# The last layer norm of a transformer block: the final 512 columns in two parts, and one of four column blocks normalised by TensorE and ScalarE

## The chip, the cores and the metric

The kernel runs on one core of a Trainium2 chip. The metric is device time in microseconds of one execution. Three runs of the kernel before took 1463.31, 1463.54 and 1463.85 us; the median is 1463.54. The core has these engines, each with a queue of its own: TensorE (PE; its weight loads are shown as PEld), VectorE (DVE), ScalarE (ACT), GpSimd (POOL) and SyncE (SP), which here only issues transfers. They meet through semaphores.

## The reference

One block of a model of width 2048 on 256 tokens, in fp32: an input projection, two attention branches, an output projection, a layer norm, a gated feed-forward network of inner width 5632, and the last layer norm. The change touches only the last line and what delivers to it:

```python
def layer_norm(x, g, b):
    xf = x.astype(jnp.float32)
    mu = jnp.mean(xf, axis=-1, keepdims=True)
    var = jnp.mean(jnp.square(xf - mu), axis=-1, keepdims=True)
    return ((xf - mu) * lax.rsqrt(var + LN_EPS) * g.astype(jnp.float32) + b.astype(jnp.float32)).astype(x.dtype)
...
        h_gate, h_up = jnp.split(x @ w_ffn_in[l], 2, axis=-1)
        x = layer_norm(DEEPNORM_ALPHA * x + (jax.nn.silu(h_gate) * h_up) @ w_ffn_out[l], ln2_g[l], ln2_b[l])
```

## The kernel before

The 256 tokens are two blocks of 128 (`tb` 0 and 1), one token per partition. The 2048 output columns of the second feed-forward product are two groups `g` of 1024, each of two halves `n` of 512; column block j = 2g + n. Each product of fp32 values is made as three matmuls on rounded parts (`mm3`, lines 207 to 209: weights' high part, weights' low part, activations' low part), and the weights are streamed and split by ScalarE (line 83, `hi`) and VectorE (line 85, `lo`).

Group 1 is the last one. Its sums grow in four PSUM banks, `bank[2 * tb + n]`. Up to the last four pairs of weight chunks, each pair is used for both token blocks (`plain_pair`, or `seven_pair` for pairs done with seven products in place of eight). The last four pairs (`HELD = 4`) are used for block 0 as they arrive and kept in SBUF. So block 0 is ready first: its two banks are added to the residual `x1[0]` and its norm `ln2(0)` runs on VectorE, while TensorE goes through the kept chunks for block 1: 24 matmuls of 512 columns into `bank[2]`, then 24 into `bank[3]`. Each bank is added to `x1[1]` by `add_out` (line 1025), which also takes the statistics of the 512 columns (`bn_stats`, line 1028, one of four sets of six numbers).

The norm itself (`ln`): VectorE aggregates the four sets to mean and variance `mv` (line 1099), makes `first(0)`, (x - mean) * gamma (line 1089), adds epsilon (`ve`, line 1101), and GpSimd raises the sum to the power -0.5 (`rs`, line 412). Then come `second(0)`, x * rs + beta (line 1094), and the same two passes for column blocks 1, 2 and 3. Each finished column block is stored, alternately by ScalarE's and SyncE's queue (line 1335). Gamma and beta come broadcast to all 128 partitions in four tiles of 1024 columns (`ln2_t`, loaded by GpSimd, line 1306, in the middle of group 1).

TensorE and SyncE run in the order in which the code is written. For VectorE, ScalarE and GpSimd a scheduler sets the order, by the code's order, priorities (`tc.high_priority`) and dependencies; within an engine nothing overtakes at run time. Dependencies on a PSUM tile are kept for the whole bank.

## Time and profile before

| what | us |
|---|---|
| runs (three) | 1463.31, 1463.54, 1463.85 |
| profiled execution, first to last instruction (its own time is not shown beside it) | 1462.0 |
| TensorE busy, share of the span | 1447.7, 99% |
| VectorE busy | 1219.6, 83% |
| ScalarE busy | 797.0, 55% |
| GpSimd busy | 45.8, 3% |
| mean granted TensorE clock | 0.998 of full speed |

Times in the profile are microseconds from the span's start. A row of the timeline gives start, duration, engine, line of the kernel, operation, output <- inputs, shape, and in brackets the idle time of the engine before it with what ended it. Records of matmuls overlap: what one costs in a stream is the distance of the starts, not the duration. A row of a group gives, behind the count, busy time in us and the mean of one in ns.

### The profile page before, as it was taken

What the parts mean: (1) busy time and instruction counts of PE and PEld (TensorE: products, weight loads), DVE (VectorE), ACT (ScalarE), POOL (GpSimd) and SP (SyncE); (2) the same over time, 40 slices, a digit from 0 to 9 for tenths busy, and PEclk for the clock granted to TensorE, in tenths of its full rate; (3) what the DMA queues carried; (4) which work ended last, traced back from release to release, by engine and by line L of the source; (5) the groups of instructions that cost most, each with busy time, mean ns of one, the idle gap of its engine ahead of it and who ended that gap; (6) DMA issues with size and microseconds to landing.
All of it is one profiled execution on the core that took longest, in us unless ns stands there. A gap on an engine that the chain in (4) does not pass through costs nothing.

```text
span 1462.0 us, 19399 instructions
## 1 busy us (share of the span) xinstructions
PE 1447.7 (99%) x7146; PEld 1217.9 (83%) x7146; DVE 1219.6 (83%) x1654; ACT 797.0 (55%) x982; POOL 45.8 (3%) x58
## 2 busy tenths in 40 slices
PE   9999999999999999999999999999999999999996
PEld 9888888888888888888888888888888888888885
DVE  6798985468489678879886799989999998989887
ACT  6765443346466445545534565656566565554551
POOL 0002010030000000000000000000000000000000
PEclk9999999999999999999999999999999999999999
DMA  8646675444556565567856767666666667888853
GB/s 295 195 155 194 185 180 169 152 135 147 186 184 217 182 208 193 185 185 245 292 182 207 239 232 245 206 211 204 228 203 211 218 215 248 311 335 267 325 199 115
DMA packets 93407, 310.16 MB, mean 212 GB/s; under 512 B 16688, under 2 KB 17624, under 8 KB 92544
## 3 DMA queue, kind: packets, MB, share of 16 engines
q1 hardware_dynamic: 82176, 290.11, 59.5%
q0 software_dynamic: 4096, 16.45, 3.5%
q10 hardware_dynamic: 7040, 2.36, 0.7%
q8 instruction: 56, 0.92, 0.3%
q14 instruction: 39, 0.32, 0.1%
HBM read 295.05 MB, written 13.83 MB: 211 GB/s over the span
## 4 chain that ended last, share of the span: by engine, by line
PE 95%; DVE 2%; DMA 1%; issue 1%; ACT 1%; SPq 0%; POOLq 0%; DVEq 0%; ACTq 0%
PE acc L145 10%; PE acc L208 10%; PE acc L209 10%; PE acc L207 10%; PE aux L207 9%; PE aux L209 9%; PE aux L208 9%; PE acc L148 5%; PE acc L167 5%; PE acc L166 5%; PE acc L165 5%; PE aux L672 1%; PE aux L165 1%; PE aux L167 1%; PE aux L166 1%
## 5 line engine op out<-in xcount | busy, mean ns | idle before, releaser
L83 ACT CAST hi<-raw 128x1024 fp32r<-128x1024 f32 (+1 forms) x391 | 405.8, 1045 | 392.1 <-PE acc L167 88.2
L85 DVE TENSOR_TENSOR lo<-raw,hi 128x1024 fp32r<-128x1024 f32 (+1 forms) x391 | 473.8, 1220 | 148.0 <-ACT hi L83 145.1
L145 PE MATMUL acc<-X,hi 128*128 128x512 f32 x640 | 203.7, 399 | 0.0
L148 PEld LDWEIGHTS acc<-X,lo 128*128 128x128 f32 x640 | 120.2, 188 | 28.3
L207 PE MATMUL acc<-hi,X 128*128 128x512 f32 x364 | 142.2, 391 | 0.0
L209 PE MATMUL acc<-hi,X 128*128 128x512 f32 x364 | 141.7, 389 | 0.0
L208 PE MATMUL acc<-lo,X 128*128 128x512 f32 x364 | 141.7, 389 | 0.0
L207 PE MATMUL aux<-hi,X 128*128 128x512 f32 x332 | 129.9, 391 | 0.6 <-DVE ol__108 L852 0.6
L209 PE MATMUL aux<-hi,X 128*128 128x512 f32 x332 | 129.3, 389 | 0.0
L208 PE MATMUL aux<-lo,X 128*128 128x512 f32 x332 | 129.2, 389 | 0.0
L148 PE MATMUL acc<-X,lo 128*128 128x256 f32 x640 | 126.0, 278 | 0.0
L145 PEld LDWEIGHTS acc<-X,hi 128*128 128x128 f32 x640 | 97.5, 189 | 2.0 <-ACT hi L83 0.7
L240 ACT CAST f_thi<-f_wt 128x1024 fp32r<-128x1024 f32 x58 | 61.1, 1054 | 52.3 <-DVE f_wt L255 30.8
L165 PE MATMUL acc<-hi,X 128*128 128x512 f32 x224 | 89.6, 400 | 0.0
L167 PE MATMUL acc<-hi,X 128*128 128x512 f32 x224 | 87.4, 390 | 0.0
L166 PE MATMUL acc<-lo,X 128*128 128x512 f32 x224 | 87.3, 390 | 0.0
L209 PEld LDWEIGHTS acc<-hi,X 128*128 128x128 f32 x364 | 68.4, 188 | 14.3
L207 PEld LDWEIGHTS acc<-hi,X 128*128 128x128 f32 x364 | 68.4, 188 | 14.0
L208 PEld LDWEIGHTS acc<-lo,X 128*128 128x128 f32 x364 | 68.3, 188 | 13.9
L241 DVE TENSOR_TENSOR f_tlo<-f_wt,f_thi 128x1024 fp32r<-128x1024 f32 x58 | 70.2, 1220 | 6.3 <-ACT f_thi L240 6.0
L207 PEld LDWEIGHTS aux<-hi,X 128*128 128x128 f32 x332 | 62.3, 188 | 13.5 <-DVE ol__108 L852 0.8
L209 PEld LDWEIGHTS aux<-hi,X 128*128 128x128 f32 x332 | 62.3, 188 | 13.0
(545 smaller groups left out, 2883.2 us busy)
## 6 DMA issues: line engine op xcount, KB each, us to landing
raw<-in_wfg_dram SPq DMA_DIRECT2D x131, 512.0 KB, 4.1
raw<-in_wws_dram SPq DMA_DIRECT2D x80, 512.0 KB, 4.1
raw<-in_wfo_dram SPq DMA_DIRECT2D x70, 512.0 KB, 5.0
raw<-in_wgt_dram SPq DMA_DIRECT2D x52, 512.0 KB, 3.6
raw<-in_win_dram SPq DMA_DIRECT2D x37, 512.0 KB, 3.7
f_wraw<-in_wfg_dram SPq DMA_DIRECT2D x29, 512.0 KB, 5.9
wraw<-in_wfo_dram SPq DMA_DIRECT2D x18, 512.0 KB, 5.1
gt<-d_g SPq DMA_DIRECT2D x18, 512.0 KB, 6.3
```

Source lines behind the costliest of these rows:

```text
L83: nc.scalar.copy(hi, raw)
L85: nc.vector.tensor_sub(lo, raw, hi.bitcast(F32))
L145: nc.tensor.matmul(pss[c], hv[:, kk, cs[c]], X2[k // 4][:, k % 4], start=(k == 0), stop=False, skip_group_check=True)
L148: nc.tensor.matmul(pss[c][:, :S], lv[:, kk, cs[c]], xh[:, k, :], start=False, stop=(k == KT - 1), skip_group_check=True)
L165: nc.tensor.matmul(ps, xh, hv[:, kk], start=(k == 0), stop=False)
L166: nc.tensor.matmul(ps, xh, lv[:, kk], start=False, stop=False)
L167: nc.tensor.matmul(ps, xl, hv[:, kk], start=False, stop=(k == 2 * n - 1))
L207: nc.tensor.matmul(o, sh, hi, start=first, stop=False)
L208: nc.tensor.matmul(o, sh, lo, start=False, stop=False)
L209: nc.tensor.matmul(o, sl, hi, start=False, stop=last)
L240: nc.scalar.copy(hi, v)
L241: nc.vector.tensor_sub(lo, v, hi.bitcast(F32))
```

## The change

For block 1 the last bank is made in two parts of 256 columns: 24 matmuls for columns 0 to 255 of the bank, addition and statistics of these, then 24 for columns 256 to 511, addition and statistics. The statistics become five sets. Epsilon is added right behind the aggregate. Column block 0 of block 1 is final since group 0; it is multiplied by gamma ahead of time. Its rest, rs * (x gamma) - mean rs gamma + beta, is made by TensorE in one PSUM bank: a product with the diagonal matrix of rs, and a product of two rows per token (-mean * rs, and 1) with the two rows gamma and beta. ScalarE makes the column mean * rs and the diagonal, copies the transposed rows out of PSUM, copies the result out of PSUM and stores it. VectorE makes the two passes for column blocks 1, 2, 3 only, all three first passes ahead of the second passes; SyncE stores these. The argument `shut` only sets the flag that closes a bank's accumulation. Block 0 is normalised as before.

```diff
@@ -219,12 +219,12 @@
         cs = slice(n * 512, (n + 1) * 512)
         mm3(bank[2 * tb + n], sh[:, k, ts], sl[:, k, ts], hi[:, cs], lo[:, cs], q == 0 and j == 0, last and j == 1)
 
-    def plain_pair(bank, src, sh, sl, q, last):
+    def plain_pair(bank, src, sh, sl, q, last, shut=None):
         cks = pair_chunks(src, q)
         for j in range(2):
             for n in range(2):
                 for tb in range(NTB):
-                    plain(bank, cks, sh, sl, q, j, n, tb, last)
+                    plain(bank, cks, sh, sl, q, j, n, tb, last or 2 * tb + n == shut)
             tick()
 
     def seven_pair(bank, wbank, src, sh, sl, q, form, home, first, last):
@@ -1020,12 +1020,13 @@
         scaled(v21, m, OP.subtract)
         nc.vector.tensor_add(v22, v22, m)
 
-    def add_out(tb, g, n, ps):
-        v = out_block(tb, g, n)
-        nc.vector.tensor_add(v, v, ps)
-        if 2 * g + n == 0:
-            stats[tb] = sm.tile([P, 4, 6], F32, name="stats", tag="stats", bufs=2)
-        nc.vector.bn_stats(stats[tb][:, 2 * g + n, :], v)
+    def add_out(tb, g, n, ps, part=slice(0, 512)):
+        v = out_block(tb, g, n)[:, part]
+        nc.vector.tensor_add(v, v, ps[:, part])
+        j = 2 * g + n
+        if j == 0:
+            stats[tb] = sm.tile([P, 5, 6], F32, name="stats", tag="stats", bufs=2)
+        nc.vector.bn_stats(stats[tb][:, j + (part.start > 0), :], v)
 
     def load_x():
         for tb in range(NTB):
@@ -1096,7 +1097,7 @@
 
         with tc.high_priority(offset=ahead[0]):
             mv = sm.tile([P, 2], F32, name="mv", tag="mv", bufs=2)
-            nc.vector.bn_aggr(mv, stats[tb].rearrange("p a b -> p (a b)"))
+            nc.vector.bn_aggr(mv, stats[tb][:, :4].rearrange("p a b -> p (a b)"))
             ve = sm.tile([P, 1], F32, name="ve", tag="ve", bufs=2)
             nc.vector.tensor_scalar(ve, mv[:, 1:2], LN_EPS, None, op0=OP.add)
             rs = sm.tile([P, 1], F32, name="rs", tag="rs", bufs=2)
@@ -1294,7 +1295,7 @@
                 if q == WQ[g][-1]:
                     start(seven_chain(g, wbank, mp_.tile([P, 512], F32, name="wm", tag="wm")))
             else:
-                plain_pair(bank, wfo[g], hh_, hl_, q, q == FT // 2 - 1)
+                plain_pair(bank, wfo[g], hh_, hl_, q, q == FT // 2 - 1, 3 if g and q == n - 1 else None)
         return bank
 
 
@@ -1335,15 +1336,59 @@
         ln(tb, Halves(*ln2_t[:2]), Halves(*ln2_t[2:]), lambda j, v: (nc.sync if j % 2 else nc.scalar).dma_start(
             out[tb * P:(tb + 1) * P, j * 512:(j + 1) * 512], v))
 
+    ts1 = slice(P, S)
+
+    def held_part(n, part):
+        for q, cks in held:
+            for j in range(2):
+                k = 2 * q + (j + n) % 2
+                cs = slice(n * 512 + part.start, n * 512 + part.stop)
+                hi, lo = cks[j]
+                last = j == 1 and q == FT // 2 - 1
+                for a, b, end in ((hh_, hi, False), (hh_, lo, False), (hl_, hi, last)):
+                    nc.tensor.matmul(bank[2 + n][:, part], a[:, k, ts1], b[:, cs], start=False, stop=end,
+                                     skip_group_check=n == 1)
+        add_out(1, 1, n, bank[2 + n], part)
+
+    gt2, bt2 = (Halves(*ln2_t[i:i + 2]) for i in (0, 2))
+    v1 = [x1[1][:, j * 512:(j + 1) * 512] for j in range(4)]
+    rows2, turn = (hp_.tile([P, 1024], F32, name=n, tag=t) for n, t in (("rows2", "hH2"), ("turn", "hL2")))
+    for i, src in enumerate((ln2g, ln2b)):
+        nc.gpsimd.dma_start(rows2[i:i + 1, :512], bass.AP(tensor=src.tensor, offset=src.offset, ap=[[0, 1], [1, 512]]))
+    ct = sm.tile([P, 2], F32, name="ct")
+    nc.gpsimd.memset(ct, -1.0)
     for n in range(2):
         add_out(0, 1, n, bank[n])
     ln2(0)
-    for n in range(2):
-        for q, cks in held:
-            for j in range(2):
-                plain(bank, cks, hh_, hl_, q, j, n, 1, q == FT // 2 - 1)
-        add_out(1, 1, n, bank[2 + n])
-    ln2(1)
+    held_part(0, slice(0, 512))
+    nc.vector.tensor_mul(v1[0], v1[0], gt2[:, slice(0, 512)])
+    held_part(1, slice(0, 256))
+    held_part(1, slice(256, 512))
+
+    mv = sm.tile([P, 2], F32, name="mv", tag="mv", bufs=2)
+    ve = sm.tile([P, 1], F32, name="ve", tag="ve", bufs=2)
+    rs = sm.tile([P, 1], F32, name="rs", tag="rs", bufs=2)
+    diag, ctT = turn[:, :P], turn[0:2, 512:512 + P]
+    with tc.high_priority(offset=LEAD):
+        nc.vector.bn_aggr(mv, stats[1].rearrange("p a b -> p (a b)"))
+        nc.vector.tensor_scalar(ve, mv[:, 1:2], LN_EPS, None, op0=OP.add)
+        rsqrt(rs, ve, hv)
+        nc.scalar.activation(ct[:, 0:1], mv[:, 0:1], AF.Copy, scale=rs)
+        nc.scalar.activation(diag, ident, AF.Copy, scale=rs)
+    y, a = ps_aux(), ps_aux()
+    nc.tensor.transpose(a[0:2, :P], ct, ident)
+    nc.scalar.activation(ctT, a[0:2, :P], AF.Copy, scale=-1.0)
+    nc.tensor.matmul(y, diag, v1[0], start=True, stop=False)
+    nc.tensor.matmul(y, ctT, rows2[0:2, :512], start=False, stop=True)
+    for j in (1, 2, 3):
+        nc.vector.scalar_tensor_tensor(v1[j], v1[j], mv[:, 0:1], gt2[:, slice(j * 512, j * 512 + 512)],
+                                       op0=OP.subtract, op1=OP.mult)
+    for j in (1, 2, 3):
+        nc.vector.scalar_tensor_tensor(v1[j], v1[j], rs, bt2[:, slice(j * 512, j * 512 + 512)],
+                                       op0=OP.mult, op1=OP.add)
+        nc.sync.dma_start(out[P:, j * 512:(j + 1) * 512], v1[j])
+    nc.scalar.copy(v1[0], y)
+    nc.scalar.dma_start(out[P:, :512], v1[0])
     assert not chains
     fh.close()
```

The order changes at three places. First, VectorE at the end of the program, from the bank ahead of the last one on (`x_1` is block 1's residual, `acc` a PSUM bank, `ln_0`, `ln_1` gamma, `ln_2`, `ln_3` beta). Before:

```order
L1025 TENSOR_TENSOR x_1_10660<-x_1_10660,acc 128x512 [waits PE_49]
L1028 BN_STATS stats<-x_1_10660 128x6 [waits DVE_49]
L1025 TENSOR_TENSOR x_1_10660<-x_1_10660,acc 128x512 [waits PE_49]
L1028 BN_STATS stats<-x_1_10660 128x6 [waits DVE_49]
L1099 BN_AGGR mv<-stats 128x2 [waits DVE_49]
L1089 SCALAR_TENSOR_TENSOR x_1_10660<-x_1_10660,mv,ln_0_11748 128x512 [waits DVE_49]
L1101 TENSOR_SCALAR ve<-mv 128x1
L1089 SCALAR_TENSOR_TENSOR x_1_10660<-x_1_10660,mv,ln_0_11748 128x512
L1094 SCALAR_TENSOR_TENSOR x_1_10660<-x_1_10660,rs,ln_2_11932 128x512 [waits Pool_49]
L1094 SCALAR_TENSOR_TENSOR x_1_10660<-x_1_10660,rs,ln_2_11932 128x512 [waits DVE_49]
L1089 SCALAR_TENSOR_TENSOR x_1_10660<-x_1_10660,mv,ln_1_11834 128x512 x2
L1094 SCALAR_TENSOR_TENSOR x_1_10660<-x_1_10660,rs,ln_3_12018 128x512 [waits DVE_49] x2
```

Now:

```order
L1025 TENSOR_TENSOR x_1_10660<-x_1_10660,acc 128x512 [waits PE_49]
L1029 BN_STATS stats<-x_1_10660 128x6 [waits DVE_49]
L1025 TENSOR_TENSOR x_1_10660<-x_1_10660,acc 128x256 [waits PE_49]
L1029 BN_STATS stats<-x_1_10660 128x6 [waits DVE_49]
L1025 TENSOR_TENSOR x_1_10660<-x_1_10660,acc 128x256 [waits PE_49]
L1029 BN_STATS stats<-x_1_10660 128x6 [waits DVE_49]
L1373 BN_AGGR mv<-stats 128x2 [waits DVE_49]
L1374 TENSOR_SCALAR ve<-mv 128x1 [waits DVE_49]
L1384 SCALAR_TENSOR_TENSOR x_1_10660<-x_1_10660,mv,ln_0_11748 128x512
L1384 SCALAR_TENSOR_TENSOR x_1_10660<-x_1_10660,mv,ln_1_11834 128x512 x2
L1387 SCALAR_TENSOR_TENSOR x_1_10660<-x_1_10660,rs,ln_2_11932 128x512 [waits DVE_49,Pool_49]
L1387 SCALAR_TENSOR_TENSOR x_1_10660<-x_1_10660,rs,ln_3_12018 128x512 [waits DVE_49] x2
```

The last addition became two of 256 columns with statistics behind each; epsilon moved ahead of the first pass; the three first passes are together, ahead of the three second passes; the passes for the first 512 columns are gone.

Second, TensorE, where the first part of the last bank ends and the second begins (`hi` and `lo` are weight parts, `hH` and `hL` the activations' parts):

```order
L1349 MATMUL acc<-hi,hL_10658 128x256
L1349 MATMUL acc<-hi,hH_10657 128x256
L1349 MATMUL acc<-lo,hH_10657 128x256
L1349 MATMUL acc<-hi,hL_10658 128x256
L1349 MATMUL acc<-hi,hH_10655 128x256 [waits DVE_49]
L1349 MATMUL acc<-lo,hH_10655 128x256
L1349 MATMUL acc<-hi,hL_10656 128x256
```

Behind the first part's last matmul stands a matmul that waits for VectorE; before, the bank's 24 matmuls of 512 columns had no wait. The end of TensorE's program is now this (`ct` the column mean * rs beside -1, `turn` the diagonal and the transposed rows, `rows` gamma and beta on two partitions):

```order
L1349 MATMUL acc<-hi,hL_10658 128x256
L1349 MATMUL acc<-hi,hH_10657 128x256
L1349 MATMUL acc<-lo,hH_10657 128x256
L1349 MATMUL acc<-hi,hL_10658 128x256
L1379 MATMUL aux<-ident,ct 2x128 [waits Activation_49]
L1381 MATMUL aux<-x_1_10660,turn 128x512 [waits Activation_49]
L1382 MATMUL aux<-rows_12418,turn 128x512 [waits DMASW3_49,DMASW2_49,Activation_49]
```

A transpose and two matmuls of 512 columns have come behind the last bank; each waits for ScalarE. The four ScalarE instructions that they need and that need them come behind ScalarE's last stores of block 0: line 1376 (`ct`), which waits for GpSimd's power, 1377 (the diagonal), 1380 and 1390 (copies out of PSUM, each waiting for TensorE), and the store of line 1391.

Third, VectorE in the middle of group 1 (weight splits and sums). Before:

```order
L241 TENSOR_TENSOR lo<-wraw,hi 128x1024 [waits Activation_49]
L241 TENSOR_TENSOR lo<-raw,hi 128x512 [waits Activation_49]
L255 TENSOR_TENSOR wt<-wt,raw 128x512 [waits DVE_49]
L241 TENSOR_TENSOR tlo<-wt,thi 128x1024 [waits Activation_49]
L251 TENSOR_TENSOR wt<-wraw,raw 128x1024 [waits DMAHW1_49,DMAHW0_49]
L85 TENSOR_TENSOR lo<-raw,hi 128x1024 [waits DMAHW6_49,Activation_49]
```

Now:

```order
L241 TENSOR_TENSOR lo<-wraw,hi 128x1024 [waits Activation_49]
L241 TENSOR_TENSOR lo<-raw,hi 128x512 [waits Activation_49]
L255 TENSOR_TENSOR wt<-wt,raw 128x512 [waits DVE_49]
L1364 TENSOR_TENSOR x_1_10660<-x_1_10660,ln_0_11748 128x512 [waits DMASW6_49]
L241 TENSOR_TENSOR tlo<-wt,thi 128x1024 [waits Activation_49]
L251 TENSOR_TENSOR wt<-wraw,raw 128x1024 [waits DMAHW1_49,DMAHW0_49]
```

The product of block 1's first column block with gamma stands in front of a split, `tlo`, that waits for ScalarE.

## The prediction

> **What bounds the kernel now.** I read the page's chain first, then TensorE, VectorE and GpSimd in the timeline from 1440 us on, then the stores. The rows below are the chain's shares from the page, and the first and the last of the 24 matmuls of the last bank (block of tokens 1, columns 1536 to 2047).
>
> ```profile
> PE 95%; DVE 2%; DMA 1%; issue 1%; ACT 1%; SPq 0%; POOLq 0%; DVEq 0%; ACTq 0%
> ...
> 1445.35 0.39 PE L207 MATMUL acc<-hi,hH 128*128 128x512 f32 x1
> ...
> 1450.57 0.39 PE L209 MATMUL acc<-hi,hL 128*128 128x512 f32 x1
> ```
>
> The chain is TensorE for 95% of the span. So only two things can move the end: when TensorE delivers the last bank, and how long the chain behind it takes. The 24 matmuls start 5.22 us apart first to last, 0.227 us each; the last ends at 1450.57 + 0.39 = 1450.96. The next rows are VectorE from the statistics of the bank before that on, with GpSimd's power.
>
> ```profile
> 1448.96 0.69 DVE L1028 BATCH_NORM_STATS2 stats<-x 128x6 f32<-128x512 f32 x1
> 1450.99 0.69 DVE L1025 TENSOR_TENSOR x<-x,acc 128x512 f32<-128x512 f32 x1 [1.34 <-PE acc L209]
> 1451.71 0.69 DVE L1028 BATCH_NORM_STATS2 stats<-x 128x6 f32<-128x512 f32 x1
> 1452.44 0.26 DVE L1099 BATCH_NORM_AGGREGATE mv<-stats 128x2 f32<-128x24 f32 x1
> 1452.74 0.75 DVE L1089 SCALAR_TENSOR_TENSOR x<-x,mv,ln 128x512 f32<-128x512 f32 x1
> 1453.40 0.15 DVE L1101 TENSOR_SCALAR ve<-mv 128x1 f32<-128x1 f32 x1
> 1453.47 0.74 DVE L1089 SCALAR_TENSOR_TENSOR x<-x,mv,ln 128x512 f32<-128x512 f32 x1
> 1454.65 1.41 DVE L1094 SCALAR_TENSOR_TENSOR x<-x,rs,ln 128x512 f32<-128x512 f32 x2 [0.44 <-POOL rs L412]
> 1455.98 1.41 DVE L1089 SCALAR_TENSOR_TENSOR x<-x,mv,ln 128x512 f32<-128x512 f32 x2
> 1457.31 1.41 DVE L1094 SCALAR_TENSOR_TENSOR x<-x,rs,ln 128x512 f32<-128x512 f32 x2
> ...
> 1453.70 0.92 POOL L412 TENSOR_TENSOR rs<-ve,hv 128x1 f32<-128x1 f32 x1 [9.47 <-DVE ve L1101]
> ```
>
> VectorE takes the last bank 0.03 us after TensorE's end and runs to 1457.31 + 1.41 = 1458.72, so the tail is 7.76 us. It is VectorE's own work (add, statistics, aggregate, eight passes over 512 columns), but for 0.44 us behind GpSimd's power. Two passes in one row take 1.41 and the next row starts 0.08 before the end: passes that follow each other are 0.665 apart. Before the last bank VectorE had 1.34 us to spare.
>
> ```profile
> L1335 SPq DMA_DIRECT2D out_dram<-x x4: 332/338/344, 1445.0 to 1458.7; - x4
> ```
>
> The last store (issues of about 0.34 us each; the last column of numbers is first and last start) is issued at 1458.7, as VectorE ends; the span ends at 1462.0, 3.28 us behind VectorE. The runs' median, 1463.54, is 1.54 above the span. I keep 3.28 and 1.54 and move only the 1458.72.
>
> **The change: TensorE's side.** The last bank is now made in two rounds of 24 matmuls of 256 columns. The built order has one new wait, in front of the first matmul of round two, for VectorE; the count it waits for is that of the addition of round one's 256 columns (same bank). That addition stands on VectorE behind everything of block 0 and behind the bank before. The nearest rows for matmuls of 256 columns, and for TensorE behind a VectorE wait, are at the program's start; the last row is an addition of 256 columns out of a bank.
>
> ```profile
> 5.52 0.39 PE L131 MATMUL acc<-X,lo 128*128 128x256 f32 x1 [0.22 <-DVE lo L85]
> 5.75 0.28 PE L128 MATMUL acc<-X,hi 128*128 128x256 f32 x1
> ...
> 6.46 0.28 PE L128 MATMUL acc<-X,hi 128*128 128x256 f32 x1
> ...
> 7.90 0.28 PE L128 MATMUL acc<-X,hi 128*128 128x256 f32 x1
> ...
> 4.77 0.69 DVE L85 TENSOR_TENSOR lo<-raw,hi 128x512 fp32r<-128x512 f32 x1 [0.96 <-ACT hi L83]
> ...
> L156 DVE TENSOR_TENSOR pre<-acc,half 128x256 f32<-128x256 f32 x20 | 8.0, 414 | 0.1
> ```
>
> From 6.46 to 7.90 are twelve matmuls: 0.120 each. Two rounds take 48 x 0.120 = 5.76 against 24 x 0.227 = 5.45: 0.31 more. VectorE's row ends at 4.77 + 0.69 = 5.46, TensorE starts at 5.52 (0.06 behind) and its second matmul comes 0.23 later (0.11 more than a step).
>
> Round one starts at 1445.35 as before, and its successor could start at 1445.35 + 24 x 0.120 = 1448.23. But VectorE reaches the round's addition only when the statistics of the bank before are through: 1448.96 + 0.69 - 0.08 = 1449.57, plus 0.414 for 256 columns = 1449.98. Round two starts at 1450.04 and ends at 1450.04 + 0.23 + 22 x 0.120 + 0.28 = 1453.19. TensorE's end moves **2.23 us later**: 1.81 of waiting, 0.31 of smaller matmuls, 0.11 of restarting. Queued behind the waiting matmul are only the rest of round two and the three new matmuls; VectorE waits for them. Before, the same lateness of VectorE cost nothing, because nobody waited for it.
>
> **VectorE's side.** Add and statistics of the second 256 columns: the statistics of 256 columns stand in no row. They lie between nothing and the 0.69 of 512; I scale them as the addition, 0.41. Add 1453.21, statistics 1453.65, aggregate 1454.09, epsilon 1454.39 (the same gaps of 0.03 to 0.04), ended at 1454.54. Epsilon first costs 0.07, as now. Then six passes, not eight, with no gap: first start 1454.46, last start 1454.46 + 5 x 0.665 = 1457.78, end 1457.78 + 0.75 = **1458.53**, 0.19 before today's 1458.72. The six are 1.33 shorter, the 0.44 wait is covered (GpSimd: 1454.54 + 0.15 + 0.92 to 1.01 = about 1455.69, before the fourth pass at 1456.45), and the second half's addition and statistics are 0.28 each shorter than a whole bank's. The sum of the savings, about 2.4, is what TensorE's 2.23 eats.
>
> The one added VectorE instruction outside the tail is the product of block 1's first 512 columns with gamma. The order puts it between the two rows that come first here:
>
> ```profile
> 1357.63 0.68 DVE L255 TENSOR_TENSOR wt<-wt,raw 128x512 f32<-128x512 f32 x1
> 1359.48 1.23 DVE L241 TENSOR_TENSOR tlo<-wt,thi 128x1024 fp32r<-128x1024 f32 x1 [1.17 <-ACT thi L240]
> ...
> 1347.67 1.08 POOL L1306 DMA_DIRECT2D ln<-in_ln2g_dram  x2 [144.56 <-PE acc L209]
> ...
> 1443.30 0.93 POOL L412 TENSOR_TENSOR rs<-ve,hv 128x1 f32<-128x1 f32 x1 [84.36 <-DVE ve L1101]
> ```
>
> There VectorE idles 1.17 us behind ScalarE, and the product takes 0.69. Gamma's load was issued at 1347.67, ten microseconds earlier. I cost it at nothing; without that cover it is 0.69 on VectorE, in a stretch where TensorE waits for nobody. The two row loads (2 KB each) and the memset go to GpSimd, which idles 84.36 us before its power at 1443.30: nothing.
>
> **ScalarE's and TensorE's new side.** The first 512 columns now leave VectorE: ScalarE makes mean times rs and diag(rs), TensorE transposes, then two fp32 matmuls of 512 columns, ScalarE copies the bank and issues the store. Prices:
>
> ```profile
> L471 ACT ACTIVATE ea<-alog 128x8 f32<-128x8 f32 x1 | 0.2, 209 | 0.7 <-DMA alog<-in_alog_dram 0.7
> L800 ACT ACTIVATE s_e<-s_e,mx 128x128 f32<-128x128 f32 x8 | 3.1, 389 | 0.0
> L155 ACT COPY half<-acc 128x256 f32<-128x256 f32 x40 | 13.1, 368 | 1.3 <-DVE lo L85 1.3
> L1213 ACT COPY v<-aux 128x512 f32<-128x512 f32 x10 | 5.6, 584 | 0.0
> L1208 PE MATMUL aux<-ident,v 128*128 128x128 f32 x40 | 5.2, 272 | 0.0
> ...
> 206.24 1.04 ACT L83 CAST hi<-raw 128x1024 fp32r<-128x1024 f32 x1 [1.77 <-PE acc L145]
> ...
> 207.39 0.30 PEld L145 LDWEIGHTS acc<-X,hi 128*128 128x128 f32 x2 [0.33 <-ACT hi L83]
> ```
>
> Small ScalarE work is 0.21, 128x128 0.39, a bank of 256 copied 0.37, of 512 0.58. TensorE starts 0.11 behind ScalarE (1.04 from 206.24 is 207.28; 207.39). From rs at 1455.69: the column 1455.73 to 1455.94; diag 1455.90 to 1456.29 (between 0.21 and the 0.58 of a full bank; 0.39 is its own shape); transpose 1456.05 to 1456.32 (0.27); its copy of 128 columns, 0.27 by the slope of 0.37 and 0.58, to 1456.63. The fp32 matmuls of 512 columns stand in no row; the nearest are these:
>
> ```profile
> 335.79 1.24 PE L672 MATMUL aux<-s_t,s_vT 128*128 128x256 f32 x5
> ...
> 323.43 1.05 PE L672 MATMUL aux<-s_t,s_vT 128*128 128x128 f32 x8
> ...
> 1.27 3.78 PE L373 MATMUL aux<-s_bm 128*128 128x128 f32 x18 [1.27 <-DVE s_bm L370]
> ```
>
> Nine warm-up matmuls (line 373) leave 18 records, so one fp32 matmul leaves two. Records of 256 columns are (1.24 - 0.38) / 4 = 0.215 apart, of 128 columns (1.05 - 0.275) / 7 = 0.111: proportional, 0.43 at 512. The two matmuls are 4 x 0.43 = 1.72, from 1456.40, plus 0.11 to start and 0.16 to drain: 1458.39. Bounds: 4 x 0.227 = 0.91 if a record ran as the other 512-column matmuls do; at the warm-up row's pace ((3.78 - 0.40) / 17 = 0.20 for 128 columns, 1.8 times as slow) 3.1, and I take 3.4 for twice as slow. The value is the proportional one, from the same kind of matmul. The copy, 1458.43 to 1459.01, now ends last, 0.48 behind VectorE and **0.29 behind today's 1458.72**. The store goes out on ScalarE's queue, the other three on SyncE's, 0.665 apart against 0.34 for an issue.
>
> **Sum.** 1462.0 + 0.29 = 1462.3 of span, 1463.54 + 0.29 = **1463.8 us**. A measurement of this kernel tells 0.2%, 2.9 us, from no change; this is no change.
>
> **Rivals.**
>
> *VectorE ends last.* If the two matmuls or ScalarE's steps are 0.5 cheaper, the end is VectorE's 1458.53: 1463.54 - 0.19 = 1463.35. For it: the 0.91 bound. Against: all fp32 rows.
>
> *TensorE's clock has halved when the new matmuls come (slower than before).* The granted clock in stretches after the last matmul, as stretch, length, five engines' busy times, then clock, DMA share and GB/s:
>
> ```profile
> 1454.00:1455.00 1.00, 0.00 (x0) 0.00 (x0) 0.56 (x2) 0.00 (x0) 0.62 (x1) 1.00 0.00 0
> 1455.00:1455.50 0.50, 0.00 (x0) 0.00 (x0) 0.50 (x2) 0.00 (x0) 0.00 (x0) 0.62 0.00 0
> 1455.50:1456.00 0.50, 0.00 (x0) 0.00 (x0) 0.50 (x2) 0.00 (x0) 0.00 (x0) 0.50 0.00 0
> ```
>
> It stays full for about 4.1 us after 1450.96, then halves. In the change TensorE idles from 1453.19 to the transpose at 1456.05, 2.9 us, after a gap of 1.65 before round two. If the clock falls before 1456.4, the two matmuls cost 1.72 more: 1459.01 + 1.72 = 1460.73, +2.01, 1465.55. It decides from 0.1 us of lost clock on, since ScalarE's copy is already last. Against it: today's 4.1 us is longer than 2.9. The Trainium skill (TensorE: Matmul & The Clock Gate, Part 1) says the gate halves after at least one free-running idle window of about 3.4 us; its Part 4 adds that transposes do not count as busy in the same way. By that rule 2.9 to 3.2 us hold no whole window and the clock stays; the trace agrees so far with its 4.1.
>
> *GpSimd and VectorE block each other.* The power now runs under VectorE passes that read two tensors. If it had to wait for the three passes, rs comes at 1456.53 + 0.92 = 1457.45, 1.76 later, and the end at +2.05, 1465.6. But at the first norm it ran under such work:
>
> ```profile
> 742.01 1.01 POOL L412 TENSOR_TENSOR rs<-ve,hv 128x1 f32<-128x1 f32 x1 [39.40 <-DVE ve L1101]
> ...
> 742.50 1.22 DVE L85 TENSOR_TENSOR lo<-raw,hi 128x1024 fp32r<-128x1024 f32 x1
> ```
>
> 1.01 instead of 0.92, and the VectorE row under it is 1.22 as its group's mean: 0.09 at most. The Trainium skill (SBUF — State Buffer, section SBUF: two separate sides) calls the shared port an exclusive lock against VectorE work with two SBUF inputs, so it speaks against this change; these two rows show no such blocking.
>
> *The new wait is already met.* If round two follows at once, TensorE ends at 1445.35 + 47 x 0.120 + 0.28 = 1451.27, 1.92 earlier, and the end is at 1459.01 - 1.92: -1.63, 1461.9. It needs VectorE to be 1.8 us ahead of its own row of 1448.96; nothing in the change makes it so.
>
> **How the numbers follow.** Forecast 0.50 (its own range 1463.4 to 1464.5, from 0.2 either way on ScalarE's steps and 0.3 of spread between runs); VectorE last 0.20; clock halved 0.13; blocked power 0.06; wait met 0.05; unnamed 0.06. The range, 1462.9 to 1465.6, runs from VectorE's end less the runs' spread to the halved clock. All named cases lie within 2.9 us of 1463.54: same 0.94. Slower, 0.04: halved clock and blocked power together (+3.8). Faster, 0.02: no wait and cheap matmuls together (VectorE's end, 1458.53 - 1.92, so -2.1) do not even reach it.
>
> **What would show it.** TensorE idle for about 1.6 us before round two with VectorE's add as releaser, the last big matmul ending near 1453.2, VectorE's last pass near 1458.5, the fp32 records 0.43 apart, the copy ending near 1459.0, PEclk 1.00 to the end of the second fp32 matmul. I am wrong if round two starts before 1449.9, if the fp32 records are 0.8 apart, or if rs comes after 1456.

## The result

| | us |
|---|---|
| kernel before, median of 4 runs (lowest, highest) | 1463.69 (1463.31, 1463.90) |
| change, median of 4 runs (lowest, highest) | 1478.29 (1477.98, 1479.21) |
| ratio, 95% interval | 1.010 (1.0088 to 1.0112) |

The change is 14.6 us slower. The forecast was 1463.8 us and its range ended at 1465.6.

The page of the change, first the span, TensorE's row and the chain's shares:

```profile
span 1476.2 us, 19469 instructions
...
PE 1464.3 (99%) x7175; PEld 1220.8 (83%) x7175; DVE 1220.1 (83%) x1655; ACT 798.3 (54%) x986; POOL 46.8 (3%) x61
...
PE 97%; DMA 1%; DVE 1%; ACT 0%; issue 0%; POOLq 0%; POOL 0%; SPq 0%; ACTq 0%; DVEq 0%
```

The span is 14.2 longer than before and TensorE's busy time grew by 16.6, for 29 records more (24 matmuls, and one transpose and two fp32 products that leave five). It is not waiting that was added. TensorE was simply at work for longer, and the chain is still TensorE.

Now the tail, in the timeline of the change, from the first matmul of the split bank on; TensorE's rows first, then VectorE's, GpSimd's and ScalarE's:

```profile
1459.01 0.28 PE L1349 MATMUL acc<-hi,hH 128*128 128x256 f32 x1
...
1463.59 0.39 PE L1349 MATMUL acc<-hi,hH 128*128 128x256 f32 x1 [1.57 <-DVE x L1025]
...
1466.41 0.28 PE L1349 MATMUL acc<-hi,hL 128*128 128x256 f32 x1
1469.57 0.27 PE L1379 MATMUL aux<-ident,ct 128*2 128x128 f32 x1 [2.88 <-ACT ct L1376]
1469.86 1.12 PE L1381 MATMUL aux<-x,turn 128*128 128x512 f32 x2
1470.91 1.12 PE L1382 MATMUL aux<-rows,turn 2*128 2x512 f32 x2
...
1466.72 0.42 DVE L1025 TENSOR_TENSOR x<-x,acc 128x256 f32<-128x256 f32 x1 [2.73 <-PE acc L1349]
1467.18 0.43 DVE L1029 BATCH_NORM_STATS2 stats<-x 128x6 f32<-128x256 f32 x1
1467.64 0.29 DVE L1373 BATCH_NORM_AGGREGATE mv<-stats 128x2 f32<-128x30 f32 x1
...
1468.04 2.07 DVE L1384 SCALAR_TENSOR_TENSOR x<-x,mv,ln 128x512 f32<-128x512 f32 x3
1470.02 2.07 DVE L1387 SCALAR_TENSOR_TENSOR x<-x,rs,ln 128x512 f32<-128x512 f32 x3
...
1468.26 0.92 POOL L412 TENSOR_TENSOR rs<-ve,hv 128x1 f32<-128x1 f32 x1 [10.48 <-DVE ve L1374]
...
1472.07 0.58 ACT L1390 COPY x<-aux 128x512 f32<-128x512 f32 x1 [1.93 <-PE aux L1382]
```

The last bank begins at 1459.01 instead of 1445.35: **13.66 us of the loss are there before the first changed matmul runs.** From there to the end of the last engine it takes 1472.65 - 1459.01 = 13.64, against 1458.72 - 1445.35 = 13.37 before: +0.27, where the prediction had +0.29.

So the loss had to be looked for where the change touches nothing. Both programs issue the same matmuls in the same order up to there, so the start of the n-th matmul can be compared in the two traces:

```
start in the kernel before, us:   44    282    561    760   1059   1258   1361   1445
later in the change by, us:     1.02   1.16   2.70   5.12   7.07   9.52  11.68  13.64
```

The delay grows without a jump. The same three stretches of both kernels, TensorE alone (stretch, length, busy time with the count of matmuls in brackets, granted clock, DMA share, GB/s), the kernel before first:

```profile
600.00:650.00 50.00, 50.00 (x230) 1.00 0.60 184
...
1340.00:1390.00 50.00, 50.00 (x222) 1.00 0.88 320
1400.00:1440.00 40.00, 40.00 (x178) 1.00 0.53 185
```

```profile
600.00:650.00 50.00, 50.00 (x223) 1.00 0.57 179
...
1340.00:1390.00 50.00, 50.00 (x216) 1.00 0.85 302
1400.00:1440.00 40.00, 40.00 (x174) 1.00 0.54 185
```

TensorE is busy throughout, at clock 1.00 in both, and gets through 2 to 3% fewer matmuls. From one 512-column matmul to the next the kernel before takes 0.227 us; in the change many steps take 0.231 to 0.238, as just ahead of the last bank:

```profile
1458.07 0.40 PE L1349 MATMUL acc<-hi,hL 128*128 128x512 f32 x1
1458.30 0.39 PE L1349 MATMUL acc<-hi,hH 128*128 128x512 f32 x1
1458.54 0.39 PE L1349 MATMUL acc<-lo,hH 128*128 128x512 f32 x1
1458.77 0.40 PE L1349 MATMUL acc<-hi,hL 128*128 128x512 f32 x1
```

Clock, waits and order are the same, so something in the matmuls themselves differs: the addresses of their operands. The pools on the left side of SBUF lie one behind the other:

```python
    cst = ctx.enter_context(tc.tile_pool(name="cst", bufs=1, side="left"))
    wp = ctx.enter_context(tc.tile_pool(name="wp", bufs=4, side="left"))
    sm = ctx.enter_context(tc.tile_pool(name="sm", bufs=1, side="left"))
```

`wp` holds `raw`, `hi` and `lo`; `sm` holds the small tiles, `stats` and the new `ct` among them; all later tiles of the left side (the hidden layer's `hH`, `hL`, the weight forms, `x1`) lie behind `sm`. `stats` grew from 96 to 120 bytes per partition, placed as 128, twice; `ct` takes 32. So everything behind `sm` moved by **96 bytes**, and `hi`, `lo` and the tiles of the right side (`X2`, `v`, `fg`, `gs`) did not. The offsets within 256 bytes at which the operands of the 512-column matmuls start, from the built programs:

```
                        hi, lo   hH, hL, f_*, g_*, thi, tlo   X2, v, fg, gs   g_form2
kernel before              128              128                    128           96
change                     128              224                    128          192
```

### The profile page after: what moved, and what is told of

Its sections match the earlier page's. It is cut to its first block, busy times and chain, and to the rows that moved or that the text cites. A ratio compares the mean times of both kernels' runs of the same rounds, so it can differ in the third digit from the quotient of the medians.

```text
span 1476.2 us, 19469 instructions
## 1 busy us (share of the span) xinstructions
PE 1464.3 (99%) x7175; PEld 1220.8 (83%) x7175; DVE 1220.1 (83%) x1655; ACT 798.3 (54%) x986; POOL 46.8 (3%) x61
## 4 chain that ended last, share of the span: by engine, by line
PE 97%; DMA 1%; DVE 1%; ACT 0%; issue 0%; POOLq 0%; POOL 0%; SPq 0%; ACTq 0%; DVEq 0%
PE acc L145 10%; PE acc L209 10%; PE acc L207 10%; PE acc L208 10%; PE aux L209 9%; PE aux L207 9%; PE aux L208 9%; PE acc L148 5%; PE acc L165 5%; PE acc L167 5%; PE acc L166 5%; DMA raw<-in_win_dram 1%; PE aux L672 1%; PE aux L166 1%; PE aux L165 1%; PE aux L167 1%
## 5 line engine op out<-in xcount | busy, mean ns | idle before, releaser
L83 ACT CAST hi<-raw 128x1024 fp32r<-128x1024 f32 (+1 forms) x391 | 405.5, 1044 | 405.8 <-PE acc L167 91.9
L207 PEld LDWEIGHTS acc<-hi,X 128*128 128x128 f32 x364 | 68.4, 188 | 14.6
L208 PEld LDWEIGHTS aux<-lo,X 128*128 128x128 f32 x332 | 62.4, 188 | 13.2
L209 PEld LDWEIGHTS aux<-hi,X 128*128 128x128 f32 x332 | 62.3, 188 | 13.2
```

Source lines behind the costliest of these rows:

```text
L83: nc.scalar.copy(hi, raw)
L207: nc.tensor.matmul(o, sh, hi, start=first, stop=False)
L208: nc.tensor.matmul(o, sh, lo, start=False, stop=False)
L209: nc.tensor.matmul(o, sl, hi, start=False, stop=last)
```

## Experiments: is it the addresses?

The first idea was an offset within 64 bytes (96 is 32 more than a multiple of 64). Four kernels, run beside the kernel before (median 1463.57).

The change whole, with 128 bytes instead of 96 added:

```diff
-    ct = sm.tile([P, 2], F32, name="ct")
+    ct = sm.tile([P, 16], F32, name="ct")[:, :2]
```

> The change whole, but the new tile ct is 64 bytes per partition instead of 8. The pool sm is then 128 bytes larger than before instead of 96, and every tile that lies behind it starts at the same offset within 64 bytes as before the change. Theory A (the added time comes from tiles that moved by 32 bytes within 64, against tiles that did not move): before the last bank nothing is left of the 13.7 us, the tail costs +0.3, so 1463.7 to 1464.2 us, with every 512-column matmul at 0.227. Rival B (the added time comes from the added work itself, in the norm or in the program's order): 1478, as the change. Rival C (any move of the tiles costs it): 1478 too.

Measured: 1478.48 (ratio 1.010, 1.0085 to 1.0116). The first idea fell.

The kernel before, with only the tile `pads`, which nobody reads, made larger, by 32 and by 64 bytes:

```diff
-    pads = sm.tile([P, 16], F32, name="pads")
+    pads = sm.tile([P, 24], F32, name="pads")
```

> The kernel before; only the unused tile pads in the pool sm is 96 bytes per partition instead of 64, so that the tiles behind it move by 32 bytes. No instruction is added but that one memset is longer. Theory A: as slow as the change without its tail, 1477.0 to 1478.5 us, with matmuls at 0.233 where moving operand and weights lie at different offsets within 64 bytes. Rival B: 1463.7.

Measured: 1475.17 (1.0078, 1.0061 to 1.0094).

```diff
-    pads = sm.tile([P, 16], F32, name="pads")
+    pads = sm.tile([P, 32], F32, name="pads")
```

> The kernel before; only the unused tile pads is 128 bytes per partition instead of 64, so that the tiles behind it move by 64 bytes. Theory A: 1463.7 within 0.3. Rival B: 1463.7. Rival C (any move): about 1478.

Measured: 1473.71 (1.0068, 1.0053 to 1.0083). An unused tile 32 bytes larger, with no other edit, costs 11.6 us; that rules out the added work as the cause of the bulk, and 64 bytes do not repair it.

All tiles to one offset, as I thought:

```diff
-    ident = cst.tile([P, P], F32, name="ident")
+    ident = cst.tile([P, P + 8], F32, name="ident")[:, 8:]
...
-    pad = padp.tile([P, 24], F32, name="pad")
+    pad = padp.tile([P, 32], F32, name="pad")
```

> The kernel before, with all its tiles moved to 32 bytes past a multiple of 64: 32 bytes ahead of ident, and 128 instead of 96 bytes in the tile pad on the other side. Moving operands and weights then lie at one offset within 64 bytes, as before, only at 32 instead of 0. Theory A, that different offsets are what costs: 1463.7 within 0.5. Rival D, that a start at 32 past 64 is slow in itself: each of some 4850 512-column matmuls costs what the slow ones of the change cost, 0.0067 us, so up to +32 us, 1478 to 1496.

Measured: 1469.13 (1.0037, 1.0024 to 1.005). The edit did not do what I meant: the right side is filled from the top, so a larger `pad` moved its tiles down, to 96, while the left went up to 160. From 1258 us on, where no operand of the right side is used any more, this kernel falls no further behind (6.58 us there, 6.62 at the last bank).

With all steps of these traces sorted by offsets, the law showed: what counts is whether moving operand and weights start at the same offset **within 256 bytes** (at one difference, 192, the step is only 1.3 ns longer). The mean step in ns from 250 us on, the two kernels and these four together, by how far the weights loaded next lie ahead of the moving operand:

```
weights ahead by, bytes      0     32     64     96    128    160    192    224
mean step, ns            227.7  233.1  232.7  233.6  233.3  233.2  229.0  233.3
matmuls                  19714   1284   1330   1272   1515    263   3175    534
```

The next four test that, beside the kernel before (median 1464.14 in this group). The change whole, with 256 bytes added instead of 96:

```diff
-    ct = sm.tile([P, 2], F32, name="ct")
+    ct = sm.tile([P, 48], F32, name="ct")[:, :2]
```

> The change whole, but the new tile ct is 192 bytes per partition instead of 8: the pool sm is 256 bytes larger than before instead of 96, and every tile behind it starts at the same offset within 256 bytes as before the change. New theory A2: TensorE's 512-column matmuls take 0.227 us where the moving operand and the weights loaded next start at the same offset within 256 bytes, and about 0.233 where they don't; then nothing of the 13.7 us is left and the tail's +0.3 shows alone: 1463.5 to 1464.3 us. Rival B (the added work or its instructions slow the whole program): 1478. Rival E (any growth of the pool costs it, by a longer period than 256 or by no period): 1470 to 1478.

Measured: 1465.61 (1.0010, 1.0001 to 1.0019). Of the 14.6 us about 13 are gone, with every added instruction still in place. The stretches as above:

```profile
600.00:650.00 50.00, 50.00 (x230) 1.00 0.60 185
...
1340.00:1390.00 50.00, 50.00 (x222) 1.00 0.88 321
1400.00:1440.00 40.00, 40.00 (x178) 1.00 0.54 184
```

The counts are those of the kernel before to the last matmul, and the last bank begins at 1445.23, 0.12 ahead of before. The 1.5 us that remain lie in the tail; they are taken up below.

The kernel before, with 256 bytes more:

```diff
-    pads = sm.tile([P, 16], F32, name="pads")
+    pads = sm.tile([P, 80], F32, name="pads")
```

> The kernel before; only the unused tile pads is 320 bytes per partition instead of 64, so that the tiles behind it move by 256 bytes. Theory A2: 1463.6 within 0.4. Rival E: 1470 to 1478, as with the moves by 32, 64, 96 and 128 bytes.

Measured: 1463.78 (1.0000, 0.9991 to 1.0009). Growth by itself costs nothing; rival E is out.

All tiles at 160, this time with the right side brought there too:

```diff
-    ident = cst.tile([P, P], F32, name="ident")
+    ident = cst.tile([P, P + 8], F32, name="ident")[:, 8:]
...
-    pad = padp.tile([P, 24], F32, name="pad")
+    pad = padp.tile([P, 80], F32, name="pad")
```

> The kernel before, with its tiles on the left moved by +32 bytes and those on the right by -224, so that both sides start at 160 instead of 128 within 256 bytes. (The run before that meant to do this moved the right side by -32, to 96, as tiles there are placed from the top down: 64 bytes lay between the sides.) Theory A2, that only the difference counts: 1463.6 within 0.6. Rival D, that an offset other than a multiple of 128 is slow by itself: all of some 4850 matmuls at 0.233, up to 1463.6 + 4850 x 0.006 = 1493.

Measured: 1463.47 (0.9997, 0.9988 to 1.0006). No offset is slow in itself; a difference is.

Steps paired with the same steps of the kernel before, up to the last bank, then account for the loss. "Unequal" means that the moving operand and the weights loaded next start at different offsets within 256 bytes:

```
kernel             512 columns, unequal     512 columns, equal      all steps
                   count   each   sum       count   each   sum      together
change              1589  6.23 ns 9.90       3887  1.10 ns 4.28      13.46 us
before +32          1569  5.93    9.31       3907  0.65    2.54      11.10
before +64          1590  4.95    7.87       3887  0.75    2.91       9.87
change, +256          60 -0.45   -0.03       5420  0.00    0.02      -0.12
```

(The rest are fp32 matmuls, those of fewer columns, and some twenty steps that wait for something; they sum to -0.7 in the change. The sums are some 0.2 us short of the delay of 13.66.) Of the delay of the change, 1.0 us is there at 44 us, where TensorE still waits for loads; in the kernels whose operands agree (+256, all at 160) that early part varies from -0.1 to 0.5, in the four of the first group from 0.6 to 0.9, and I did not settle how much of it is the addresses'.

## Experiments: TensorE alone

Does it need the other engines' traffic to the same memory? And is it really the weights loaded *next*? This kernel leaves the block out and copies x to the output; 27 lines of 96 matmuls each, after 96 that wake TensorE:

```diff
+    for i in range(96): nc.tensor.matmul(ps[i // 3 % 8], W(0, i), M(0, i, 512), start=True, stop=True)
+    for i in range(96): nc.tensor.matmul(ps[i // 3 % 8], W(32, i), M(0, i, 512), start=True, stop=True)
...
```

> A kernel that leaves the whole block out and writes x to the output; it measures TensorE alone. After 96 matmuls that wake it, each line runs 96 fp32r matmuls that switch among four weights and four moving operands. Lines differ only in where these start within 256 bytes: first the weights at 0 to 224 in steps of 32 with the moving operand at 0; then the moving operand at 32 to 224 with the weights at 0; both at 32, 96 and 128; weights at 4, 8 and 16; two lines in which weights and moving operand take 0 and 32 in turn, once so that each matmul's own pair agrees (and its moving operand differs from the weights loaded next), once so that the moving operand agrees with the weights loaded next; at the end 256 columns with weights at 0, 32, 128 and 192. No other engine works meanwhile. Theory A2: 0.227 us from one matmul to the next where moving operand and next weights agree within 256 bytes, 0.232 to 0.234 where not (about 0.229 for weights 192 ahead); of the two turns the first is slow and the second fast. Rival F: it is the matmul's own weights that count, so the first turn is fast and the second slow. Rival G: the slow pitch needs the other engines' and the queues' traffic to the same memory; then every line of 512 columns stands at one pitch.

The groups of some lines, as count, busy time in us, and the mean of one in ns: weights at 32 (L83), at 128 (L86), at 192 (L88), both at 32 (L97), both at 0 (L82):

```profile
L83 PE MATMUL acc<-mov,wts 128*128 128x512 f32 x96 | 22.6, 395 | 0.0
...
L86 PE MATMUL acc<-mov,wts 128*128 128x512 f32 x96 | 22.5, 394 | 0.0
...
L88 PE MATMUL acc<-mov,wts 128*128 128x512 f32 x96 | 22.1, 391 | 0.0
...
L97 PE MATMUL acc<-mov,wts 128*128 128x512 f32 x96 | 22.0, 389 | 0.0
...
L82 PE MATMUL acc<-mov,wts 128*128 128x512 f32 x96 | 21.9, 389 | 0.0
```

And the mean step of every line, from the starts in the trace, in ns:

```
offset, bytes                      0      32     64     96     128    160    192    224
weights at it, moving at 0       226.7  233.3  233.4  234.2  232.3  233.4  229.0  233.3
moving at it, weights at 0              233.4  229.0  233.5  233.4  234.2  233.2  233.3
both at it                              227.1         227.1  226.9
weights at 4, 8, 16; moving at 0:  232.4, 230.7, 233.3
0 and 32 in turn, own pair equal: 231.8;  next pair equal: 233.3
256 columns, weights at 0, 32, 128, 192; moving at 0:  119.9, 118.3, 118.7, 117.8
```

The law holds with TensorE alone, so rival G is out. It holds for 4 bytes. And the two lines in turn are both slow: neither the own nor the next pair alone decides. One look further, at single matmuls that differ among equal ones:

```diff
+    for i in range(192): nc.tensor.matmul(ps[i // 3 % 8], W(32 * (i % 8 == 0), i), M(0 * (i % 8 == 0), i, 512), start=True, stop=True)
...
```

> A kernel like e9_offsets (the block is left out, x is written to the output; TensorE alone works): ten lines of 192 fp32r matmuls of 512 columns. All operands start at 0 within 256 bytes, but in every eighth matmul one or two differ: none; the weights at 32, at 128, at 192; the moving operand at 32, at 128; both at 32 in the same matmul; the moving operand at 32 and the weights of the matmul behind it at 32; the weights at 32 and the moving operand of the matmul behind it; the moving operand at 32 and the weights two matmuls later. Read by place in the eight. Theory A2 (the moving operand against the weights loaded next, one matmul ahead): one weights tile at 32 lengthens one step, that of the matmul ahead of its own, by 0.006 us, and leaves the seven others at 0.227; one moving operand at 32 lengthens its own step; moving operand and next weights both at 32 cost nothing. Rival J (loads run further ahead, or a difference sets back the stream for some matmuls): the excess is spread over two or more steps, and no pair of the four costs nothing.

```
mean step in ns from matmul          7 to 0  0 to 1  1 to 2  2 to 3  3 to 4  4 to 5  5 to 6  6 to 7   excess
none differs                           227.0   226.7   226.7   226.7   226.7   226.7   226.7   226.7       0
weights of 0 at 32                     234.9   228.3   232.5   230.9   226.7   226.7   226.7   226.7      19
weights of 0 at 128                    232.0   234.3   226.7   226.7   226.7   226.7   226.7   226.7      12
weights of 0 at 192                    225.8   236.0   228.3   232.3   231.0   226.7   226.6   226.7      19
moving operand of 0 at 32              227     236     234     232     231     227     226     227        26
moving operand of 0 at 128             227.3   234     226     226     227     227     226     227         6
weights and moving operand of 0 at 32  234.7   230.0   238.3   232.4   230.9   226.7   226.7   226.7      32
moving of 0, weights of 1 at 32        227.0   235.7   233.3   231.0   226.7   226.7   226.7   226.7      20
weights of 0, moving of 1 at 32        234.6   228.4   230.0   232.4   235.9   228.3   232.5   230.9      39
moving of 0, weights of 2 at 32        230.7   236     235     224     231     235.7   228.3   232.7      39
```

A weights tile at 32 or 128 lengthens the step ahead of its own matmul, as theory A2 had it (at 192 the first long step is the next one). But one difference sets back up to four steps, 19 to 26 ns in all at 32 bytes, and no pairing is free: a moving operand and the next weights that differ together cost 20 where the two apart cost 39. That is rival J. It also explains most of why the "equal" steps of the change are 1.1 ns longer: sorted by tile names, about 2.8 us of their excess stand in the four steps behind an unequal one and 0.9 in the next three. The last 0.9 us, some 0.3 ns in each of the others, are not explained by this. What inside the memory or TensorE needs these steps to recover, the runs do not show.

## Experiments: the tail

With the addresses out of the way, the change still stood 1.5 us above before, not 0.3. Its tail in `e5`'s trace (the change with 256 bytes added):

```profile
1445.23 0.28 PE L1349 MATMUL acc<-hi,hH 128*128 128x256 f32 x1
...
1452.76 0.28 PE L1349 MATMUL acc<-hi,hL 128*128 128x256 f32 x1
...
1456.21 2.08 PE L1381 MATMUL aux<-x,turn 128*128 128x512 f32 x2
...
1458.22 2.07 PE L1382 MATMUL aux<-rows,turn 2*128 2x512 f32 x2
...
1460.33 0.59 ACT L1390 COPY x<-aux 128x512 f32<-128x512 f32 x1 [3.83 <-PE aux L1382]
```

```profile
1455.80:1456.00 0.20, 0.08 (x1) 0.08 (x1) 0.20 (x1) 0.20 (x2) 0.00 (x0) 1.00 0.00 0
1456.00:1456.20 0.20, 0.19 (x1) 0.00 (x0) 0.20 (x1) 0.16 (x1) 0.00 (x0) 0.90 0.00 0
1456.20:1456.40 0.20, 0.19 (x1) 0.19 (x2) 0.20 (x2) 0.17 (x1) 0.00 (x0) 0.50 0.00 0
```

The second fence is stretches with the busy times of TensorE, its loads, VectorE, ScalarE and GpSimd, then the granted clock, DMA share and GB/s. The clock halves at 1456.2, as the two fp32 products begin; each takes 2.0 us instead of the 1.05 of the change's own trace, and the copy ends 1460.92 - 1445.23 = 15.69 behind the last bank's start instead of 13.64. The change with 128 bytes added shows the same (15.56); its clock fell already at 1468.4:

```profile
1468.20:1468.40 0.20, 0.00 (x0) 0.00 (x0) 0.20 (x1) 0.00 (x0) 0.20 (x1) 0.95 0.00 0
1468.40:1468.60 0.20, 0.00 (x0) 0.00 (x0) 0.20 (x1) 0.05 (x1) 0.12 (x1) 0.50 0.00 0
```

The runs of this one kernel say the same: of the eleven with 256 bytes added, the eight whose mean granted clock was 0.997 took 1465.41 to 1466.16 us, and the only one at 0.999 took 1463.48.

Then the change without the split, to see what the split itself is worth:

```diff
     held_part(0, slice(0, 512))
     nc.vector.tensor_mul(v1[0], v1[0], gt2[:, slice(0, 512)])
-    held_part(1, slice(0, 256))
-    held_part(1, slice(256, 512))
+    held_part(1, slice(0, 512))
...
-    ct = sm.tile([P, 2], F32, name="ct")
+    ct = sm.tile([P, 48], F32, name="ct")[:, :2]
...
-        nc.vector.bn_aggr(mv, stats[1].rearrange("p a b -> p (a b)"))
+        nc.vector.bn_aggr(mv, stats[1][:, :4].rearrange("p a b -> p (a b)"))
```

> As e5_change_256, but the final 512 columns in one part, as before the change: TensorE waits for nothing there. The block done by TensorE and ScalarE and the epsilon added at once stay. By the rows of before and of the change, TensorE's last bank ends when it did before, VectorE's tail lacks two passes of 0.69 us and ends some 1.8 us earlier than before, and the path over ScalarE and TensorE ends some 0.5 us behind it: 1461.9 to 1462.6 us, about 1.4 below before. If the split is what makes the tail short, it is 1463.7 or more.

Measured: 1463.99 (1.0001, 0.9992 to 1.001), no difference, where 1.4 less was expected. That is the figure foretold for the case that the split makes the tail short, but the trace shows another reason. VectorE's part came as worked out; ScalarE's did not:

```profile
1450.34 0.39 PE L1349 MATMUL acc<-hi,hL 128*128 128x512 f32 x1
...
1454.40 2.07 PE L1380 MATMUL aux<-x,turn 128*128 128x512 f32 x2
1454.57 2.07 DVE L1386 SCALAR_TENSOR_TENSOR x<-x,rs,ln 128x512 f32<-128x512 f32 x3
...
1458.51 0.58 ACT L1389 COPY x<-aux 128x512 f32<-128x512 f32 x1 [3.73 <-PE aux L1381]
```

VectorE is done at 1456.64, 2.1 ahead of before (0.2 of it because the last bank begins that much earlier), and the end waits for the products at half clock. If that is the cause, matmuls that keep TensorE at work through its wait must give it back. They read tiles that are there and write a bank that nobody reads; 11 in the change, 13 without the split:

```diff
+    keep = ps_aux()
+    for i in range(11):
+        nc.tensor.matmul(keep, hh_[:, 2 * held[0][0], ts1], held[0][1][0][0][:, :512], start=True, stop=True)
     y, a = ps_aux(), ps_aux()
```

> As e5_change_256 (the change, with the tiles at the offsets of before), and 11 matmuls of 512 columns into a bank that nobody reads, right behind TensorE's last bank: 2.5 us of its wait of some 3.0 us for ScalarE. In the profile of e5_change_256 the granted clock fell to 0.50 at 1456.2 us, and the two products took 4.1 us instead of 2.1. Theory H (that clock made the tail 2.0 us longer than the sum): the clock stays 1.00 through the products, and the time is that of the kernel before, +0.3: 0.1 to 0.7 above it, where e5_change_256 stood 1.5 above. Rival I (something else in the tail): as e5_change_256, 1.4 above before.

> As e8_no_split (the change without the split, tiles at the offsets of before), and 13 matmuls of 512 columns into a bank that nobody reads behind TensorE's last bank: 2.95 us of its wait of 3.4 us. Theory H: the clock stays 1.00, the copy ends at about 1457.1 instead of 1459.1 us, VectorE at 1456.6: 1.3 to 1.8 us below the kernel before. Rival I: as e8_no_split, no different from before.

```profile
1452.96 2.68 PE L1380 MATMUL aux<-hi,hH 128*128 128x512 f32 x11
...
1457.35 1.12 PE L1385 MATMUL aux<-rows,turn 2*128 2x512 f32 x2
1458.51 0.59 ACT L1393 COPY x<-aux 128x512 f32<-128x512 f32 x1 [1.93 <-PE aux L1385]
```

These rows are the change with 11, and a stretch of it:

```profile
1457.00:1458.00 1.00, 1.00 (x3) 0.29 (x2) 1.00 (x3) 0.00 (x0) 0.00 (x0) 1.00 0.00 0
```

The clock stays 1.00, and a product takes 1.05 again. The rows without the split, with 13:

```profile
1454.75 2.07 DVE L1389 SCALAR_TENSOR_TENSOR x<-x,rs,ln 128x512 f32<-128x512 f32 x3
...
1456.80 0.58 ACT L1392 COPY x<-aux 128x512 f32<-128x512 f32 x1 [1.93 <-PE aux L1384]
```

```
from the last bank's first matmul to the end of the last engine, us     span     median (before beside it)
kernel before                           13.37                         1462.0
change                                  13.64                         1476.2   1478.29 (1463.69)
change, +256 bytes                      15.69   clock halved          1464.2   1465.61 (1464.14)
the same, TensorE kept at work          13.79                         1462.6   1464.70 (1463.82)
+256 bytes, no split                    13.97   clock halved          1462.4   1463.99 (1464.14)
the same, TensorE kept at work          12.08                         1460.9   1463.24 (1463.82)
```

Theory H is borne out by the traces: the added matmuls keep the clock and shorten the tail by 1.9 both times, and the mean granted clock is 0.999 or 1.000 in all eleven runs of each. The margin is small: in the two traces the clock fell 0.4 and 0.3 us behind the end of the products. The times alone would not show it. Both medians miss what theory H gave, 0.9 above before where it had 0.1 to 0.7, and 0.6 below where it had 1.3 to 1.8, and runs of one kernel lie 1.6 to 3 us apart in these groups: the change kept at work is at 1.0007 of before (0.9998 to 1.0015), the one without the split at 0.9994 (0.9985 to 1.0003). The tail of the latter is 1.29 shorter than before and its span 1.1; the median is 0.6 lower, which the runs cannot tell from nothing. No version here clearly beats the kernel before.

## Why the prediction was wrong

**The step that failed is in what was costed at nothing.** The sum lets the last bank start where it did, "Round one starts at 1445.35 as before", and it started at 1459.01. The product with gamma, the row loads and the memset were named, each with its cover, and these did cost nothing: with 256 bytes added, all of them still run and the last bank begins 0.12 earlier than before. Not named were the tiles. `stats` with a fifth row and `ct` were taken as room without a price, and their 96 bytes brought the operands of 1589 matmul steps to unequal offsets. That cost 13.5 us by the steps, 9.9 of it in these and 4.3 in other 512-column steps (the rest is -0.7), nearly five times the 2.9 that the prediction held to be measurable. No rival held it, so 0.94 for "same" rested on a list of work alone. The kernel had a hint: `pad` and `pads` are two tiles that nobody reads, and with them every operand but `g_form2` started at 128 within 256 bytes.

The Trainium skill (SBUF — State Buffer, section Operand start alignment) requires only that an operand starts at a multiple of its element size, and says itself that this is about legality and that its runs timed nothing. All offsets here obey it, and the step still differs between 226.7 and 234.2 ns.

**The tail came out as forecast in the profiled run, in part by luck.** The steps up to the products are right by their mechanism. On the clock of before (the trace less 13.66):

| step | predicted | measured |
|---|---|---|
| round two starts, behind VectorE's addition | 1450.04 | 1449.93 |
| TensorE's idle time there | about 1.6 | 1.57 |
| last big matmul ends | 1453.19 | 1453.03 |
| `rs` there | 1455.69 | 1455.52 |
| VectorE ends | 1458.53 | 1458.43 |
| fp32 records apart | 0.43 | 0.53 |
| copy ends | 1459.01 | 1458.99 |

Two errors cancel in the last row: the products began 0.2 earlier, and their records were each 0.1 further apart. And the products ran at full clock only because it fell at 1472.0, as they ended: with the same instructions and 128 or 256 bytes added, it fell before or as they began, and the tail took 15.56 and 15.69 instead of 13.64. The stores took 0.27 longer to the span's end than the 3.28 I kept (3.55; 3.50 and 3.52 in the two kernels kept at work, 3.28 and 3.31 where the copy ended 2 us later than VectorE's); why, the runs do not show.

**The rival of the halved clock had the right mechanism, nearly the right price (1.72 for the two products, 1.9 in the traces) and too small a chance.** It put the time 2.0 above before; with its operands at equal offsets the change is 2.2 above in span and 1.5 in the median, so that 1465.61 stands so near to the 1465.55 of the prediction is luck. Four traces have the products behind an idle TensorE: in three the clock fell before or as they began, in the change's own as they ended. The argument against it, that today's 4.1 us are longer than 2.9, took one trace's delay for a limit. From TensorE's last big matmul to the fall it was 3.12 and 3.05 in two of the three and 2.36 in the one with 128 bytes added. In the kernel before, where nothing follows that matmul, it was 4.2, and in its five variants 2.0, 2.0, 2.6, 4.0 and 4.5. One of the two shortest, the kernel before with 256 bytes added to `pads`:

```profile
1450.04 0.39 PE L209 MATMUL acc<-hi,hL 128*128 128x512 f32 x1
...
1452.20:1452.40 0.20, 0.00 (x0) 0.00 (x0) 0.18 (x1) 0.00 (x0) 0.00 (x0) 1.00 0.00 0
1452.40:1452.60 0.20, 0.00 (x0) 0.00 (x0) 0.20 (x1) 0.00 (x0) 0.00 (x0) 0.55 0.00 0
```

What varies can be read from the clock's records in the twelve traces of whole kernels. The stretch at full clock lasted 1447.25, 1450.66, 1454.08, 1457.49, 1460.90 or 1467.73 us: each is a whole multiple of 3.4133, between 424 and 430 of them. So the fall comes on a grid of 3.413 us that begins with the rise, and the delay depends on where on it TensorE's last big matmul ends. The Trainium skill (TensorE: Matmul & The Clock Gate, Part 1) lets the gate fall after an idle window of some 3.4 us that runs free. The grid agrees with a window that runs free, since idling does not restart it; falls after 2.0 and 2.4 us of idling do not agree with a whole idle window, since such a window would have to hold 1.4 and 1 us of matmuls.

**The other rivals.** VectorE last: it ended 0.56 ahead of the copy. Blocked power: GpSimd's row is 0.92 under VectorE's three passes of line 1384, 1468.04 to 1470.1, so it did not wait. Wait met: it was 1.57.

## What to carry to other kernels

A tile that is added or resized moves every tile behind it in its side of the memory, so compare the operands' start addresses before and after as one compares the order; here moving operands and weights of long matmul streams had to agree within 256 bytes, and 56 bytes of new data per partition cost 1% of a kernel until the pool was padded to a multiple of 256. When a delay grows without a jump over a program that was changed only at its end, count matmuls per stretch at equal clock before looking for a wait. And a short chain over TensorE behind an idle time of 2 us or more can run at half clock (the fall came 2.0 to 4.5 us after the last big matmul), so both prices belong in the sum, or TensorE is kept at work.

## What was not expected of the hardware

- A 512-column fp32r matmul takes 226.7 ns from the next where operands agree within 256 bytes, and 231 to 234 where they differ by as little as 4 bytes; 229.0 where the moving operand lies 64 ahead of the weights. One odd operand among equal ones sets back up to four steps, 6 to 26 ns in all.
- With 256 columns it is the other way round: 119.9 ns where they agree, 117.8 to 118.7 where not. In the kernel with 64 bytes between the sides, 864 such matmuls were 1.1 ns faster each than before, 0.96 us in all.
- The granted clock halved 2.0 to 4.5 us after TensorE's last big matmul, in nine traces that idle there; the stretch at full clock ended on a grid of 3.413 us in all twelve.
